# A two-layer decoder trunk on one core: the last sliding-window softmax of a layer in two halves, and the row roots by another pair of products

## The chip, the core and the metric

The kernel runs on one core of one Trainium2 chip. The time is the device time in microseconds (us) of one execution. The core has five engines that each work through a list of instructions of their own in order: PE (matrix products), DVE (vector work on tiles), ACT (functions and scaled copies), POOL (a further vector engine, which here also issues some DMAs) and SP (which only issues DMAs). They wait for each other through semaphores. PE writes its products into PSUM, which is cut into banks of 128 partitions by 512 numbers; a bank must be read out ("evicted") by DVE or ACT before PE can write new products into it.

## The reference

A trunk of two layers over one sequence of 256 tokens with 1024 channels. In each layer the normalised input is multiplied by one wide matrix, three mixers work on the pieces, each mixer's result is gated and projected back, and the sum is added to the residual:

```python
for layer in range(DEPTH):
    h = rms_norm(x, norm_w[layer])
    proj = jnp.einsum('bsd,de->bse', h, w_in[layer])
    (a_xbc, a_z, a_dt, b_q, b_k, b_v, b_z,
     c_q, c_k, c_v, c_f, c_z, gates) = jnp.split(proj, split_at, axis=-1)
    y_a = mamba2_branch(...)
    y_b = sliding_window_branch(b_q, b_k, b_v, b_z, sinks[layer], cos, sin)
    y_c = forgetting_attention_branch(...)
    ys = jnp.stack([y_a, y_b, y_c], axis=2)
    branch = jnp.einsum('bsiw,iwd->bsid', ys, w_proj[layer])
    g = jax.nn.sigmoid(gates.reshape(b, s, N_BRANCH, d) + gate_bias[layer])
    merged = jnp.sum(g * branch, axis=2)
    x = x + jnp.einsum('bsd,de->bse', merged, w_out[layer])
return rms_norm(x, final_norm_w)
```

The sliding-window mixer has 16 query heads in 4 groups, a window of 128 keys and one extra score per head (the sink) that takes part in the softmax and has no value:

```python
scores = jnp.einsum('bnqkgd,bnskd->bnkgqs', qb, kb) * (HEAD_DIM ** -0.5)
mask = band[None] & (key_pos >= 0)
scores = jnp.where(mask[None, :, None, None], scores, -jnp.inf)
probs = jax.nn.softmax(jnp.concatenate([scores, sink], axis=-1), axis=-1)[..., :-1]
out = jnp.einsum('bnkgqs,bnskd->bnqkgd', probs, vb)
```

With 256 tokens there are two query blocks of 128. The queries of block 0 see only the keys of block 0 (128 columns of scores), those of block 1 see the keys of both blocks, but never more than 128 of them at once.

## The kernel before

**Products.** To reach float32 accuracy with PE's faster number form, every weight is split in two parts, hi (a rounded copy, line 293, ACT) and lo (weight minus hi, line 294, DVE), and so is the normalised input (hTh, hTl). A weight arrives from memory by a DMA that SP issues (tile raw), in parts of 128x1024 numbers; each part costs one ACT copy and one DVE subtraction. Six raw tiles and six split tiles are in turn, and the planner lets four parts be held at a time. All products go through line 109 (mm); transposes through line 113.

**Units.** The wide matrix is worked through in units that the program text lists one after another. Three sorts matter here. A convolution or gate-path unit of 256 columns has 16 products into one bank. It is evicted by two ACT copies (lines 489 and 490), after which a DMA that POOL issues (line 491) adds one onto the other. For a convolution unit an ACT scaled copy (line 829), three DVE taps (line 832), an ACT tanh (line 838) and a DVE product (line 839) follow. A gate unit of 512 columns has 24 products and is evicted by one DVE addition of the bias (line 1102) and an ACT tanh (line 1105). A projection unit has 24 products of a mixer's split result with w_proj. These units take their banks in turn from a pool of three ("mm"); scores, transposes and small products take theirs from another pool ("mx").

**Side work.** Softmaxes, transposes and products with values are written as Python generators. A planner's clock (clock["t"]) advances with each product by an assumed cost; `yield 3.0` in a generator means that it goes on when this clock is 3 later, at the end of a unit. A `yield` therefore sets where on PE's list the next piece of side work stands. DVE's and ACT's lists follow from a scheduler that orders instructions by priority in program order and by assumed costs, except where an instruction is pinned (`issue_after` holds instructions back until a named one has been issued).

**The sliding softmax.** attn_quad (from line 586) handles four heads of one group, a quad. Its scores lie in four mx banks: columns 0:128 are block 0, columns 128:384 block 1. Block 0 takes a masked reduction per head on DVE (line 618), which also writes the tile pp, and an exponential per head on ACT (line 613). Block 1 takes a predicated copy, which folds the two key blocks into 128 columns (line 626), a maximum (line 627), a minimum with the sink for two heads (line 631), and an exponential per head. After that each block has its sink's part of the sum (lines 637 to 639), a reciprocal (641) and a product over four heads (642). Then the four transposes of block 0 with one ACT copy, `yield D_SOFT2` with D_SOFT2 = 3, the four transposes of block 1 with two DVE products (lines 678 and 679), then `yield D_EVAC`. For the second and the fourth quad the products with the values follow for two quads at once: 8 into an mx bank and 8 into an mm bank, each evicted by a DVE product with the gate path (line 726). The results are split into hi and lo again and feed the projection of this mixer.

In layer 0 the fourth quad's softmax lies at 141 to 147 us of the span, while PE works on a gate unit; ten units of 256 columns follow, and behind them the projection unit. Layer 1 does the same 395 us later.

**Row roots.** At the start of layer 0 (normalize, line 1388) each token's 1/rms must stand along the free axis. Two ACT copies (line 1392) scale the identity matrix's rows by it; two float32 products of 128 columns with a matrix of ones spread the diagonal over all partitions; four DVE products (line 1402) multiply the input by it, and four splits into hTh and hTl follow.

Of the kernel before, what the change touches and what calls it, by code (L numbers as in the profile page):

```python
# [16 lines left out]
P = 128  # L17
# [14 lines left out]
D_FOLD = 8.0  # L32
N_RAW, N_SPLIT = 6, 6
# [17 lines left out]
def hybrid_trunk(  # L51
# [238 lines left out]
    def split(hi, lo, src, scale=None, keep=lambda f: f):  # L290

        if scale is None:
            keep(act)(hi, src, AF.Copy)  # L293
            keep(tt)(lo, src, hi.bitcast(F32), op=ALU.subtract)  # L294
# [91 lines left out]
    def feed(i=-1):  # L386

        lim = state["limit"]
        while state["split"] < len(stream) and state["split"] != lim and (
# [7 lines left out]
            else:  # L397
                split(hi, lo, raw, keep=keep)
# [187 lines left out]
    def attn_quad(y, last, products, biases, nsink, v, vcols, sz, gated, scored=lambda: None, window=False):  # L586
# [29 lines left out]
        for h in range(4) if window else ():  # L616
            own = pps[0][:, h // 2, h % 2 * P:h % 2 * P + P]
            nc.vector.tensor_tensor_reduce(  # L618
                out=own, in0=scs[h][:, 0:P], in1=wmask, scale=-0.125, scalar=nsink[:, h:h + 1],
                op0=ALU.add, op1=ALU.min, accum_out=nm[:, h:h + 1])  # L620
            chances(h, 0, own)
        for h in range(4) if window else ():


            own = scs[h][:, 2 * P:3 * P]
            nc.vector.copy_predicated(own, wmask.bitcast(mybir.dt.uint32), scs[h][:, P:2 * P])
            nc.vector.tensor_reduce(nm[:, 4 + h:5 + h], own, axis=mybir.AxisListType.X, op=ALU.max)
            if h % 2 == 1:
                hs = slice(h - 1, h + 1)
                nh = slice(3 + h, 5 + h)  # L630
                stt(nm[:, nh], nm[:, nh], -0.125, nsink[:, hs], op0=ALU.mult, op1=ALU.min)
                for i in (h - 1, h):
                    chances(i, 1, scs[i][:, 2 * P:3 * P])
        for b in range(2) if window else ():
# [7 lines left out]
            tt(of_heads(b), of_heads(b), bc(rs.rearrange("p (i j) -> p i j", i=2), 3, P), op=ALU.mult)  # L642
        for p in () if window else range(2):
# [22 lines left out]
        if window:  # L666
            first, both = T("L4", [P, 2, 512]), T("L2", [P, 512])
            for b in range(2):
                if b == 1:
# [718 lines left out]
    def normalize(y):  # L1388

        rb = T("L1", [P, S])  # L1390
        for t in range(2):
            act(rb[:, t * P:(t + 1) * P], ident, AF.Copy, scale=y.rn[:, t:t + 1])
# [27 lines left out]
    with tc.manual_schedule(engines={ENG.PE, ENG.DVE, ENG.Activation, ENG.Pool}):  # L1420
# [119 lines left out]
        y0.rn = rsqrt(v, 2, r0)  # L1540

# [42 lines left out]
```

## Time and profile before

| | |
|---|---|
| median of 3 runs | 807.94 us (807.66 to 808.07) |
| the profiled execution's own time | 808.24 us |
| its span | 806.5 us (1.74 us lie around it) |
| granted TensorE clock | 0.999 |
| busy: PE, DVE, ACT, POOL | 99%, 85%, 66%, 21% |
| instructions on DVE, ACT | 1414, 1144 |

PE's busy time is counted from the start of an instruction to its modelled end, and the records of successive products overlap. So a short wait of PE is read better from the distance between the starts of two products: a product of 512 columns is followed by the next start 0.22 us later when nothing waits, one of 256 columns by 0.11 us. A row "x2" of a timeline holds two instructions that stand without idle time between them.

### The profile page before, as it was taken

To read this page: it belongs to the slowest core of one execution; us is meant where nothing else is said; L and a number is where in the kernel's file an instruction comes from. 1 tells how busy PE (TensorE), PEld (TensorE's weight loads), DVE (VectorE), ACT (ScalarE), POOL (GpSimd) and SP (SyncE) were. 2 spreads that over 40 slices of the span, in tenths; PEclk is the share of its full clock that TensorE was granted. 3 is DMA by queue.
4 is the path that set the end of the run, shared out by engine and by line. 5 is a ranking of instruction groups with operands and counts; after the bars stand their busy time and mean duration, and the time that the engine had idled before them with its cause. 6 is when DMAs were issued, how large, how long until landed. Compare 5 with 4: busy or idle time off the path is not lost.

```text
span 806.5 us, 14832 instructions
## 1 busy us (share of the span) xinstructions
PE 797.2 (99%) x5162; PEld 711.2 (88%) x5162; DVE 684.8 (85%) x1414; ACT 533.7 (66%) x1144; POOL 170.9 (21%) x238
## 2 busy tenths in 40 slices
PE   8999999999999999999999999999999999999996
PEld 7998988888888988888998899888889989888896
DVE  6868999998899997795785799999879999969865
ACT  7776768875776785543665678687747768755452
POOL 3156213130320100033001741222212110002000
PEclk9999999999999999999999999999999999999999
DMA  9998987797665565676678987689986646576632
GB/s 313 268 266 178 248 222 195 212 295 226 161 212 172 170 192 171 220 249 210 215 245 259 235 206 225 158 217 281 267 229 184 194 147 200 157 248 210 210 109 75
DMA packets 138826, 170.43 MB, mean 211 GB/s; under 512 B 9352, under 2 KB 106464, under 8 KB 138752
## 3 DMA queue, kind: packets, MB, share of 16 engines
q1 hardware_dynamic: 114960, 140.53, 55.3%
q0 software_dynamic: 13328, 13.29, 10.3%
q10 hardware_dynamic: 10464, 15.67, 6.7%
q8 instruction: 41, 0.67, 0.3%
q14 instruction: 33, 0.27, 0.1%
HBM read 154.71 MB, written 2.16 MB: 195 GB/s over the span
## 4 chain that ended last, share of the span: by engine, by line
PE 97%; DVE 1%; DMA 1%; issue 0%; ACT 0%; SPq 0%
PE mm L109 84%; PE mx L109 10%; PE mx L113 3%; DMA raw<-in_w_in_dram 1%; DVE lo L294 0%; DVE L L1102 0%; SPq L189 0%; DVE L L1446 0%; ACT L L1450 0%; ACT hi L1459 0%; ACT L L1226 0%; DVE L L1201 0%; SPq L363 0%; DVE L L1205 0%; DVE L L288 0%
## 5 line engine op out<-in xcount | busy, mean ns | idle before, releaser
L109 PE MATMUL mm<-L,hi 128*128 128x512 f32 x1056 | 354.0, 387 | 0.7 <-DVE L L1102 0.5
L294 DVE TENSOR_TENSOR lo<-raw,hi 128x1024 fp32r<-128x1024 f32 (+1 forms) x276 | 312.4, 1151 | 43.8 <-ACT hi L293 41.1
L293 ACT ACTIVATE hi<-raw 128x1024 fp32r<-128x1024 f32 (+1 forms) x276 | 265.9, 982 | 60.3 <-PE mm L109 38.2
L109 PE MATMUL mm<-hi,L 128*128 128x512 f32 (+2 forms) x1168 | 303.4, 349 | 0.1
L109 PE MATMUL mm<-L,lo 128*128 128x256 f32 x1056 | 266.6, 273 | 0.0
L109 PEld LDWEIGHTS mm<-hi,L 128*128 128x128 f32 x1168 | 205.7, 190 | 23.1 <-issue 1.5
L109 PEld LDWEIGHTS mm<-L,hi 128*128 128x128 f32 x1056 | 194.9, 190 | 27.3 <-issue 4.9
L109 PEld LDWEIGHTS mm<-L,lo 128*128 128x128 f32 x1056 | 202.1, 191 | 5.4
L109 PE MATMUL mm<-lo,L 128*128 128x512 f32 (+2 forms) x584 | 201.6, 347 | 0.0
L109 PEld LDWEIGHTS mm<-lo,L 128*128 128x128 f32 x584 | 110.2, 190 | 11.0 <-DVE lo L294 0.3
L491 POOL DMA_DIRECT2D L<-L x68 | 60.3, 911 | 191.9 <-ACT L L490 180.2
L1071 POOL TENSOR_SCALAR_AFFINE_SELECT bias<-bias 128x128 f32<-128x128 f32 x64 | 33.4, 555 | 77.2 <-DMA bias<-cumd 77.2
L832 DVE SCALAR_TENSOR_TENSOR L<-L,vec,L 128x255 f32<-128x255 f32 (+2 forms) x96 | 46.2, 481 | 2.1 <-ACT L L829 0.3
L489 ACT ACTIVATE L<-mm 128x256 f32<-128x256 f32 x84 | 32.0, 381 | 19.5 <-PE mm L109 14.1
L655 ACT ACTIVATE pp<-pp,nm 128x128 f32<-128x128 f32 x64 | 28.2, 443 | 22.1 <-DVE nm L649 22.1
L1105 ACT ACTIVATE L<-L 128x512 f32<-128x512 f32 x24 | 15.1, 630 | 35.7 <-DVE L L1102 31.2
L491 POOL DMA_DIRECT2D qt<-L x16 | 13.8, 862 | 76.3 <-ACT qt L490 76.3
L613 ACT ACTIVATE pp<-pp,nm 128x128 f32<-128x128 f32 x32 | 12.6, 394 | 25.6 <-DVE nm L618 24.9
L1138 POOL TENSOR_TENSOR L<-L,L 128x512 f32<-128x512 f32 x8 | 12.0, 1496 | 73.9 <-DVE L L1137 73.9
L490 ACT ACTIVATE L<-mm 128x256 f32<-128x256 f32 x68 | 26.2, 386 | 1.2 <-DMA L<-L 1.2
L1102 DVE TENSOR_TENSOR L<-mm,L 128x512 f32<-128x512 f32 x22 | 15.1, 686 | 11.7 <-PE mm L109 9.1
L838 ACT ACTIVATE L<-L 128x256 f32<-128x256 f32 x32 | 13.4, 418 | 16.5 <-DVE L L832 16.4
(212 smaller groups left out, 918.3 us busy)
## 6 DMA issues: line engine op xcount, KB each, us to landing
raw<-in_w_in_dram SPq DMA_DIRECT2D x191, 512.0 KB, 5.2
raw<-in_w_proj_dram SPq DMA_DIRECT2D x48, 512.0 KB, 6.2
L<-L POOLq DMA_DIRECT2D x72, 128.0 KB, 5.4
raw<-in_w_out_dram SPq DMA_DIRECT2D x16, 512.0 KB, 4.8
bias<-cumd ACTq DMA_DIRECT2D x16, 256.0 KB, 3.2
L<-cumd ACTq DMA_DIRECT2D x8, 512.0 KB, 6.5
L<-in_gate_bias_dram ACTq DMA_DIRECT2D x12, 256.0 KB, 5.9
qt<-L POOLq DMA_DIRECT2D x16, 128.0 KB, 6.0
```

What stands on the lines that cost most here:

```text
L109: nc.tensor.matmul(o, a, b, **kw)
L113: nc.tensor.transpose(o, a, i)
L293: keep(act)(hi, src, AF.Copy)
L294: keep(tt)(lo, src, hi.bitcast(F32), op=ALU.subtract)
L489: act(halves(lo), ordered(p[:, S:2 * S]), AF.Copy)
L490: last = act(halves(out), ordered(p[:, 0:S]), AF.Copy)
L491: nc.gpsimd.dma_start(out, lo, accum_op=ALU.add)
L655: act(pp[:, i, sl], pp[:, i, sl], AF.Exp, scale=-1.0, bias=nm[:, e:e + 1], accum_out=sums[:, e:e + 1])
L832: stt(a[:, s:S], x_[:, 0:S - s], y.vec[:, 16 * j + u:16 * j + u + 1], a[:, s:S], op0=ALU.mult, op1=ALU.add)
L1071: nc.gpsimd.affine_select(out=bias[:, i, dst], in_=bias[:, i, src], compare_op=ALU.is_ge, fill=NEG, base=0, pattern=[[-1, P]], channel_mul ...
L1102: tt(halves(g), p, halves(y.gb), op=ALU.add)
L1105: finish(act(g, g, AF.Tanh, scale=0.5))
```

## The change

It has two parts that do not touch each other.

The row roots: 1/rms is split in two parts (rparts: a DVE copy into the faster number form, and a DVE subtraction for the rest). Four ACT copies scale the identity by them, and two products of 256 columns with the ones in the faster form add up in one bank. The wait ahead of the products is `yield 4.0` in place of `yield 2.0`.

The softmax: in the sliding mixer's last quad of a layer (`apart`), only block 0 is computed at first. After block 0's transposes the generator waits `D_LATER` = 1.5; then block 1's part (later_block) and its normalisation are issued, held behind the latest lo split of a weight at that point; after a further `D_FOLD` = 8 come block 1's transposes. The first three quads of a layer are computed as before.

```diff
+D_LATER = 1.5
 ...
             keep(act)(hi, src, AF.Copy)
-            keep(tt)(lo, src, hi.bitcast(F32), op=ALU.subtract)
+            return keep(tt)(lo, src, hi.bitcast(F32), op=ALU.subtract)
 ...
-                split(hi, lo, raw, keep=keep)
+                state["latest"] = split(hi, lo, raw, keep=keep)
 ...
+        apart = window and last
+
+        def later_block():
+            for h in range(4):
+                own = scs[h][:, 2 * P:3 * P]
+                nc.vector.copy_predicated(own, wmask.bitcast(mybir.dt.uint32), scs[h][:, P:2 * P])
+                nc.vector.tensor_reduce(nm[:, 4 + h:5 + h], own, axis=mybir.AxisListType.X, op=ALU.max)
+                if h % 2 == 1:
+                    hs = slice(h - 1, h + 1)
+                    nh = slice(3 + h, 5 + h)
+                    stt(nm[:, nh], nm[:, nh], -0.125, nsink[:, hs], op0=ALU.mult, op1=ALU.min)
+                    for i in (h - 1, h):
+                        chances(i, 1, scs[i][:, 2 * P:3 * P])
+
+        if window:
+            if not apart:
+                later_block()
+            for b in range(1 if apart else 2):
+                normalize_block(b)
 ...
             for b in range(2):
-                if b == 1:
+                if b == 1 and apart:
+                    yield D_LATER
+                    with tc.issue_after(state["latest"].ins):
+                        later_block()
+                        normalize_block(1)
+                    yield D_FOLD
+                elif b == 1:
                     yield D_SOFT2
 ...
-        rb = T("L1", [P, S])
+        rb = [T("L1", [P, S], F32R) for _ in range(2)]
         for t in range(2):
-            act(rb[:, t * P:(t + 1) * P], ident, AF.Copy, scale=y.rn[:, t:t + 1])
-        yield 2.0
+            for o, r in zip(rb, y.rparts):
+                act(o[:, t * P:(t + 1) * P], ident, AF.Copy, scale=r.bitcast(F32)[:, t:t + 1])
+        yield 4.0
         p = pmx()
-        for t in range(2):
-            mm(p[:, t * P:(t + 1) * P], ones, rb[:, t * P:(t + 1) * P], start=True, stop=True)
+        for i in range(2):
+            mm(p[:, 0:S], onesr, rb[i], start=(i == 0), stop=(i == 1))
 ...
         y0.rn = rsqrt(v, 2, r0)
+        y0.rparts = [T("rparts", [P, 2], F32R, bufs=2) for _ in range(2)]
+        nc.vector.tensor_copy(y0.rparts[0], y0.rn[:, 0:2])
+        tt(y0.rparts[1], y0.rn[:, 0:2], y0.rparts[0].bitcast(F32), op=ALU.subtract)
```

The function normalize_block(b) holds the lines 637 to 642 of before unchanged. Line numbers of after are one higher than before up to line 612. In the softmax 618 becomes 629, 626/627/631 become 638/639/643, and 637/639/641/642 become 620/622/624/625; behind it 678/679 are 693/694, 726 is 741, 832/839 are 847/854, 940 is 955, 1102 is 1117 and 1402 is 1418.

How the lists of the engines change is shown for DVE at three places. In the rows, lo is the low part of a weight, mm and mx are PSUM banks, the number behind a name tells one tile from another, and L1, L2, L8, L16 are working tiles.

The first place is layer 0's last quad, from the gate unit's first eviction on. Before:

```order
L1102 TENSOR_TENSOR L2_409_2027<-mm_396_1942,L2_395_1940 128x512
L641 RECIPROCAL rsum_406_2005<-sums_400_1958 128x4
L639 TENSOR_TENSOR sums_400_1958<-sums_400_1958,es_407_2008 128x4
L642 TENSOR_TENSOR pp_397_1955<-pp_397_1955,rsum_406_2005 128x2x256
L641 RECIPROCAL rsum_408_2012<-sums_400_1958 128x4
L642 TENSOR_TENSOR pp_398_1956<-pp_398_1956,rsum_408_2012 128x2x256
L940 TENSOR_SCALAR L8_182_905<-L1_410_2030,L8_182_905 128x256
L294 TENSOR_TENSOR lo_419_2065<-raw_371_1837,hi_418_2064 128x1024
L294 TENSOR_TENSOR lo_422_2077<-raw_374_1851,hi_421_2076 128x1024
L294 TENSOR_TENSOR lo_437_2139<-raw_388_1914,hi_436_2138 128x1024
L1102 TENSOR_TENSOR L2_424_2082<-mm_411_2033,L2_395_1940 128x512
L294 TENSOR_TENSOR lo_440_2153<-raw_391_1928,hi_439_2152 128x1024
```

After, from the sink's part of block 0 on:

```order
L622 TENSOR_TENSOR sums_403_1965<-sums_403_1965,es_408_1994 128x4
L624 RECIPROCAL rsum_409_1998<-sums_403_1965 128x4
L625 TENSOR_TENSOR pp_400_1962<-pp_400_1962,rsum_409_1998 128x2x256
L1117 TENSOR_TENSOR L2_410_2013<-mm_399_1949,L2_398_1947 128x512
L955 TENSOR_SCALAR L8_185_912<-L1_411_2016,L8_185_912 128x256
L295 TENSOR_TENSOR lo_420_2051<-raw_374_1844,hi_419_2050 128x1024
L295 TENSOR_TENSOR lo_423_2063<-raw_377_1858,hi_422_2062 128x1024
L295 TENSOR_TENSOR lo_438_2125<-raw_391_1921,hi_437_2124 128x1024
L1117 TENSOR_TENSOR L2_425_2068<-mm_412_2019,L2_398_1947 128x512
L295 TENSOR_TENSOR lo_441_2139<-raw_394_1935,hi_440_2138 128x1024
L638 COPY_PREDICATED mx_404_1966<-wmask_9_88,mx_404_1966 128x128
L847 TENSOR_SCALAR L1_426_2071<-L1_381_1870,vec_181_901,L1_426_2071 128x255
```

Block 0 alone is now finished ahead of the first gate eviction (L1117), the three lo splits and the second eviction follow as before, and block 1's predicated copies and maxima (L638, L639) come behind the fourth lo split, among the taps of a convolution unit (L847).

The second place is around the products with the values. Before, from the products with the masks behind block 1's transposes to the eviction of the values' two banks (L726):

```order
L839 TENSOR_SCALAR L8_377_1862<-L1_443_2162,L1_430_2115 128x256
L678 TENSOR_TENSOR L4_431_2120<-mx_447_2187,other_10_89 128x512
L679 TENSOR_TENSOR L2_432_2121<-mx_447_2187,tri_5_76 128x512
L294 TENSOR_TENSOR L8_503_2449<-L8_182_905,L8_502_2448 128x2x256
L294 TENSOR_TENSOR lo_468_2294<-raw_420_2068,hi_467_2293 128x1024
L832 TENSOR_SCALAR L1_457_2228<-L1_426_2090,vec_178_894,L1_457_2228 128x255
L294 TENSOR_TENSOR L8_503_2449<-L8_182_905,L8_502_2448 128x2x256
L832 TENSOR_SCALAR L1_457_2228<-L1_426_2090,vec_178_894,L1_457_2228 128x254
L294 TENSOR_TENSOR lo_471_2308<-raw_423_2080,hi_470_2307 128x1024
L832 TENSOR_SCALAR L1_457_2228<-L1_426_2090,vec_178_894,L1_457_2228 128x253
L726 TENSOR_SCALAR L8_182_905<-mx_463_2263,L8_182_905 128x512
L726 TENSOR_SCALAR L8_182_905<-mm_464_2272,L8_182_905 128x512
```

After, from just behind the first product with a mask (L693) to the second eviction of the values (L741):

```order
L847 TENSOR_SCALAR L1_464_2258<-L1_435_2114,vec_181_901,L1_464_2258 128x254
L694 TENSOR_TENSOR L2_433_2107<-mx_475_2300,tri_5_76 128x512
L847 TENSOR_SCALAR L1_464_2258<-L1_435_2114,vec_181_901,L1_464_2258 128x253
L295 TENSOR_TENSOR lo_483_2352<-raw_442_2142,hi_482_2351 128x1024
L854 TENSOR_SCALAR L8_380_1869<-L1_474_2297,L1_464_2258 128x256
L295 TENSOR_TENSOR lo_498_2429<-raw_454_2208,hi_497_2428 128x1024
L847 TENSOR_SCALAR L1_486_2361<-L1_460_2233,vec_181_901,L1_486_2361 128x255
L741 TENSOR_SCALAR L8_185_912<-mx_487_2366,L8_185_912 128x512
L847 TENSOR_SCALAR L1_486_2361<-L1_460_2233,vec_181_901,L1_486_2361 128x254
L295 TENSOR_TENSOR lo_501_2443<-raw_457_2222,hi_500_2442 128x1024
L847 TENSOR_SCALAR L1_486_2361<-L1_460_2233,vec_181_901,L1_486_2361 128x253
L741 TENSOR_SCALAR L8_185_912<-mm_488_2375,L8_185_912 128x512
```

Between the product with the second mask and the second eviction of the values' banks stood two lo splits and three taps, and two splits of results (L294 128x2x256). Now three lo splits, four taps and one product L854 stand there, and the two evictions are no longer neighbours.

On PE the transposes of block 1 stand five units behind those of block 0 (two before), the products with the values two units after that (two before), and the projection unit two units later (four before). So the order of units is the same, and the side work stands three units later among them. On ACT the exponentials of block 1 stand two units of 256 columns later, and two DMA issues of cumd (line 861) move behind them; on POOL two DMA issues of line 491 stand ahead of the masks of the forgetting mixer (line 1071). SP's list is the same.

The third place is the normalisation at the start of layer 0. Before:

```order
L294 TENSOR_TENSOR lo_67_349<-raw_52_274,hi_66_348 128x1024
L294 TENSOR_TENSOR lo_70_367<-raw_53_276,hi_69_366 128x1024
L1402 TENSOR_TENSOR L8_23_130<-L8_23_130,mx_72_373 128x512 x3
L294 TENSOR_TENSOR L16_73_376<-L8_23_130,L16_73_376 128x4x128
L1402 TENSOR_TENSOR L8_23_130<-L8_23_130,mx_72_373 128x512
L294 TENSOR_TENSOR L16_73_376<-L8_23_130,L16_73_376 128x4x128 x3
L294 TENSOR_TENSOR lo_77_429<-raw_54_278,hi_76_428 128x1024
```

After:

```order
L295 TENSOR_TENSOR lo_70_356<-raw_54_278,hi_69_355 128x1024
L295 TENSOR_TENSOR lo_73_374<-raw_55_280,hi_72_373 128x1024
L295 TENSOR_TENSOR lo_80_436<-raw_56_282,hi_79_435 128x1024
L1418 TENSOR_TENSOR L8_23_130<-L8_23_130,mx_76_406 128x512 x3
L295 TENSOR_TENSOR L16_77_409<-L8_23_130,L16_77_409 128x4x128 x3
L1418 TENSOR_TENSOR L8_23_130<-L8_23_130,mx_76_406 128x512
L295 TENSOR_TENSOR lo_83_454<-raw_57_284,hi_82_453 128x1024
L295 TENSOR_TENSOR L16_77_409<-L8_23_130,L16_77_409 128x4x128
```

The third lo split of the next weight piece (raw_54 before, raw_56 after) stands ahead of the four products by the row roots (L1402, now L1418) instead of behind them and the four splits of the input; the fourth lo split stands ahead of the input's last one.

More of the change, by code (lines that the diff above doesn't have):

```diff
@@ L614, in chances, with normalize_block @@
                 bias=nm[:, e:e + 1], accum_out=sums[:, e:e + 1])
[L616 to L634, printed above, removed]
+        def normalize_block(b):
             hs = slice(4 * b, 4 * b + 4)
```

6 lines of the change are left out of this document (added).

## The prediction

> **What bounds the kernel now.** I read the page first, then PE's waits, then the distances between the starts of products on PE's timeline, and only where PE stands did I look at the engine that it waits for. The page's busy shares, its chain and PE's waits:
>
> ```profile
> span 806.5 us, 14832 instructions
> PE 797.2 (99%) x5162; PEld 711.2 (88%) x5162; DVE 684.8 (85%) x1414; ACT 533.7 (66%) x1144; POOL 170.9 (21%) x238
> PE 97%; DVE 1%; DMA 1%; issue 0%; ACT 0%; SPq 0%
> PE mm L109 <- DVE L L1102: 0.5, 1, 0.5
> ```
>
> PE is the bound, 97% of the chain is its own. So the time changes by the products that PE is given or spared, and by moments in which a product waits. Most of DVE's and ACT's work is free as long as it is in time. The change adds no product but in the normalisation; what it can move are PE's waits. The timeline of PE shows these beside the change, layer 0 and then layer 1:
>
> ```profile
> 150.97 0.38 PE L109 MATMUL mm<-L,hi 128*128 128x512 f32 x1
> 151.88 0.45 PE L109 MATMUL mm<-L,hi 128*128 128x512 f32 x1 [0.53 <-DVE L L1102]
> 152.17 0.38 PE L109 MATMUL mm<-L,lo 128*128 128x256 f32 x2
> ...
> 546.40 0.98 PE L109 MATMUL mm<-L,hi 128*128 128x512 f32 x2
> 547.22 0.38 PE L109 MATMUL mm<-L,lo 128*128 128x256 f32 x2
> ```
>
> With 0.22 us between starts as usual, the product at 151.88 should have started at 151.19: 0.69 us lost. In layer 1 two products with 0.22 each should bring the next row at 546.84, or 546.91 with the 0.07 by which the product at 151.88 takes longer too (0.29 to the next row): 0.31 lost. Both are the first product of a 256-column unit. Its bank was last used by the second gate unit, whose eviction (L1102) stands late in DVE's list. DVE's and ACT's timelines of layer 0 show why:
>
> ```profile
> 144.98 0.69 DVE L1102 TENSOR_TENSOR L<-mm,L 128x512 f32<-128x512 f32 x1
> 146.55 3.89 ACT L293 ACTIVATE hi<-raw 128x1024 fp32r<-128x1024 f32 x4
> 147.63 3.50 DVE L294 TENSOR_TENSOR lo<-raw,hi 128x1024 fp32r<-128x1024 f32 x3
> 151.05 0.68 DVE L1102 TENSOR_TENSOR L<-mm,L 128x512 f32<-128x512 f32 x1
> ```
>
> The softmax holds the first L1102 back to 144.98. On ACT the tanh of that eviction stands ahead of the four hi copies (146.55), the first lo needs the first copy's end (about 147.6, a quarter of 3.89 later), three lo splits take 3.42, and only then comes the second L1102; PE starts 0.83 after it.
>
> **The row roots.** Rows of PE, DVE and ACT at the start:
>
> ```profile
> 20.82 0.61 PE L109 MATMUL mx<-L,ones 128*128 128x128 f32 x4
> 21.19 0.47 PE L109 MATMUL mm<-hi,L 128*128 128x256 f32 x2
> 21.49 0.28 PE L109 MATMUL mm<-lo,L 128*128 128x256 f32 x1
> 21.60 0.39 PE L109 MATMUL mm<-hi,L 128*128 128x256 f32 x2
> ...
> 29.22 0.59 PE L109 MATMUL mm<-hi,L 128*128 128x512 f32 x2
> 29.74 0.48 PE L109 MATMUL mm<-lo,L 128*128 128x512 f32 x1
> 30.06 0.59 PE L109 MATMUL mm<-hi,L 128*128 128x512 f32 x2
> ...
> 28.47 4.75 DVE L294 TENSOR_TENSOR lo<-raw,hi 128x1024 fp32r<-128x1024 f32 x6
> ...
> L1392 ACT ACTIVATE L<-ident,rs 128x128 f32<-128x128 f32 x2 | 0.7, 402 | 0.0
> ```
>
> The two float32 products of before hold PE for 0.37 (20.82 to 21.19), and the pair behind them takes 0.30 instead of 0.22, so 0.45. The new two have 256 columns in the faster form, as the products at 21.49 have at 0.11 each: 0.22. The gain is 0.15 by the distance alone and 0.23 with the slow pair; I take 0.2. The Trainium skill ("FP8 and Floating Point Precision", TensorE Precision Notes) says that true float32 takes four passes through the array; four records for what the program writes as two products show only two for each, so the trace doesn't settle the number of passes. By four passes of 128 columns, at the 55.8 ns that "TensorE: Matmul & The Clock Gate" (Wait — 56ns) gives for one, it would be 0.45 before and 0.23 gained, an estimate at my upper value.
>
> Two more ACT copies (0.4 each) lie ahead of a hi copy, and two tiny DVE instructions ahead of the lo splits; PE needs neither within a unit, and the extra unit of delay covers them. Without that cover they would cost at most their 0.8. The moved third lo split is worth more. The row at 29.74 comes 0.52 after the one before it where two products take 0.43, and the next 0.32 after a single one where 0.22 is usual: 0.19 lost waiting for the split that starts at 28.47, behind the normalisation. After, it stands ahead of the normalisation and is long done. The next one has to follow seven normalisation instructions instead of eight and a split; I put its end at about 30.3, and PE wants it at 30.7. The early part sums to -0.39, between -0.15 (if the fourth split eats the 0.19) and -0.42.
>
> **The softmax, up to the second gate eviction.** The steps of the first block:
>
> ```profile
> 141.32 0.35 DVE L618 CUSTOM_DVE_ANT_0 pp<-mx,wmask,nsink 128x128 f32<-128x128 f32 x1
> 142.71 0.39 ACT L613 ACTIVATE pp<-pp,nm 128x128 f32<-128x128 f32 x1
> 143.09 0.39 ACT L613 ACTIVATE pp<-pp,nm 128x128 f32<-128x128 f32 x1
> ...
> 142.93 0.49 DVE L626 COPY_PREDICATED mx<-wmask,mx 128x128 f32<-128x128 uint32 x2
> 143.33 0.48 DVE L627 TENSOR_REDUCE nm<-mx 128x1 f32<-128x128 f32 x2
> 143.73 0.15 DVE L631 SCALAR_TENSOR_TENSOR nm<-nm,nsink 128x2 f32<-128x2 f32 x1
> ```
>
> Without block 1, DVE has done its four reductions by about 142.5. The exponentials follow each other by 0.38 on ACT from 141.7 on and end at about 143.4; sink, sum and reciprocal (0.5 with the handing over) and the product (0.6) bring the first L1102 to 144.5, 0.48 earlier. DVE idles there, because it waits for ACT. All that hangs on the chain moves by the same 0.48: lo splits from 147.15, second L1102 at 150.57, PE at 151.4. The stall is 0.2 instead of 0.69: a gain of 0.48.
>
> **The softmax, after that.** Here DVE pays back what it didn't do. Durations and windows:
>
> ```profile
> 152.00:165.00 13.00, 13.00 (x96) 11.25 (x97) 12.11 (x19) 10.74 (x23) 4.03 (x5) 1.00 0.97 274
> 165.00:177.00 12.00, 12.00 (x75) 10.99 (x74) 11.13 (x19) 9.45 (x20) 4.83 (x9) 1.00 1.02 300
> ...
> 155.48 1.52 DVE L832 SCALAR_TENSOR_TENSOR L<-L,vec,L 128x255 f32<-128x255 f32 x3
> 156.97 2.36 DVE L294 TENSOR_TENSOR lo<-raw,hi 128x1024 fp32r<-128x1024 f32 x2
> 159.24 0.42 DVE L839 SCALAR_TENSOR_TENSOR L<-L,L 128x256 f32<-128x256 f32 x1
> 159.58 0.68 DVE L678 TENSOR_TENSOR L<-mx,other 128x512 f32<-128x512 f32 x1
> 160.18 0.68 DVE L679 TENSOR_TENSOR L<-mx,tri 128x512 f32<-128x512 f32 x1
> ...
> 154.99 0.42 DVE L839 SCALAR_TENSOR_TENSOR L<-L,L 128x256 f32<-128x256 f32 x1 [0.55 <-ACT L L838]
> 172.58 1.23 DVE L294 TENSOR_TENSOR lo<-raw,hi 128x1024 fp32r<-128x1024 f32 x1 [0.27 <-ACT hi L293]
> 176.82 0.43 DVE L839 SCALAR_TENSOR_TENSOR L<-L,L 128x256 f32<-128x256 f32 x1 [0.54 <-ACT L L838]
> ...
> 165.77 0.42 ACT L838 ACTIVATE L<-L 128x256 f32<-128x256 f32 x1 [1.65 <-DVE L L832]
> ...
> 176.30 0.59 PE L109 MATMUL mm<-hi,L 128*128 128x512 f32 x2
> ```
>
> The columns of the windows are length, then busy time of PE, PEld, DVE, ACT and POOL. DVE is busy for 23.24 of the 25 us up to the projection unit, so it has 1.76 of slack. From one start to the next, a lo split takes 1.14, a tap 0.4 to 0.5, a product of 512 columns 0.60, L839 0.34, a predicated copy 0.20, a maximum 0.20, L631 0.15.
>
> The list of after goes on at 152.3, behind the fourth lo split: four copies, four maxima, two minima and a sink difference (2.1) with the six taps of two units (2.8) and two L839 (0.7), whose second waits for ACT, since its tanh stands behind block 1's exponentials. That gives 158.15; then sum, reciprocal and product of block 1 (0.95), so the next weight's first lo starts at about 159.15. Before, it started at 156.97: DVE is 2.2 late, because it idled while ACT did block 0 and now does block 1 where it has little slack.
>
> From 159.15 to the end of the values' second eviction (L741) I count eight lo splits (9.1), nine taps (3.6 at 0.4), two 512-wide splits, two L694-type products and two evictions (6 by 0.6, 3.6) and two L854 (0.7): 17.0, so 176.1 if nothing waits. I add 0.5 for a lo split behind its hi copy, since ACT must run a tanh and evict two units in front of it, and 0.2 for taps back to back: 176.9 with the write's tail. PE's first product of the projection unit needs this bank, and starts 0.14 later (the distance from an eviction's end to PE at 151.88): 177.03. Without any stall PE would be there at 176.30 - 0.69 = 175.61. So layer 0 loses 1.42 in place of 0.69, **+0.73**. In between PE also meets the lateness at a unit whose bank ACT evicts late and at the second value products, but these lie within the 1.42, not on top of it.
>
> Layer 1 has the same DVE list, and PE stands 0.38 later against it, the difference of 0.69 and 0.31. It loses 1.04 in place of 0.31, **+0.73** again. With no wait at all the sum is 176.33, 0.72 lost in layer 0 and 0.34 in layer 1: +0.03 each, the lower bound. With three waits as before (0.55, 0.27, 0.54) in place of my 0.7 it is 0.66 more, +1.39 each, the upper bound.
>
> The rest I cost at nothing: two DMAs of cumd go out later on ACT's queue, and POOL's masks stand behind two more DMA issues. They serve the scan and the forgetting mixer, which begin only behind the projection unit, and POOL is busy for 21%. If that cover were gone, PE would wait at the first of those mixers' products.
>
> **The sum.** -0.39 + 0.73 + 0.73 = +1.07. The profiled execution is 808.24 (span and 1.74 around it), 0.30 above the median of the runs; on the median 807.94 this gives **809.0**. About 0.2% (1.6 us) is what a measurement of this kernel can tell from no change.
>
> **The rivals.** (a) DVE keeps up: block 1's work fits into the slack and the stalls vanish in both layers, -0.69 - 0.31 - 0.39: 806.55. For it speaks that the split takes 2.2 us of DVE work out of the place where PE is waiting. Against it: the slack of 1.76 lies behind ACT's answers (the 0.54 and 0.27 waits), not where the work is put. It decides if the values' second eviction ends before 175.5. This is the faster side. (b) ACT holds the rest. Its row at 165.77 stood 1.65 idle for a DVE tap, with all evictions of units queued behind it. If DVE is later, such a wait grows, delays the eviction of PE's banks and the next hi copy, hence the next lo and the next tap. I price one such round at 0.6 per layer over mine: 810.2; it decides if a third tap ends over 0.5 later than I have it. The Trainium skill ("PSUM — Partial Sum Buffer", Engine vs sequencer instructions) calls the queues of ScalarE and VectorE strict FIFO, and the idle ahead of 165.77, with ready evictions behind it, agrees with that. (c) Only the first stall shrinks and DVE is just in time later, the lower bound of the sum: 0.06 - 0.39, 807.6.
>
> **How the numbers follow.** My forecast, with 808.4 to 809.5 as its own range, gets 0.40; (b) 0.32, since my count contains only one wait and the list has many; (c) 0.14; (a) 0.14. Slower by over 0.2% (above 809.55) takes (b) and a little of mine: 0.35. Faster by over 0.2% (below 806.3) needs more than (a) gives: 0.09. The rest is 0.56. The range from 807.0 to 810.7 leaves out most of (a) below and a second round of (b) above.
>
> **What would show it.** In the profile after: PE's products with the ones at about 23.5, twice 256 columns, no gap near 29.7; PE's stall at 151 down to 0.2; DVE with over 1 us idle between 142 and 147; the second L741 ending at about 177 with PE's first projection product right behind it, at 177.03 less the 0.39 of the early gain. I am wrong if DVE reaches that eviction before 176, or if PE waits anywhere past the projection unit.

## The result and the profile after

The changed kernel takes 809.14 us (median of 22 runs, 808.59 to 809.57), the kernel before, run beside it, 807.97 us (22 runs). The ratio is 1.0015, with a 95% interval from 1.0009 to 1.0021: slower by 0.7 to 1.7 us. The 1.17 us between the medians is under the 0.2% that the prediction set as the least that tells, but the whole interval lies above 1. The profiled execution took 808.95 us, its span is 807.2.

The page of the changed kernel:

```profile
PE 797.2 (99%) x5160; PEld 711.4 (88%) x5160; DVE 684.4 (85%) x1416; ACT 533.2 (66%) x1146; POOL 174.2 (22%) x238
PE 88%; DVE 6%; issue 2%; ACT 2%; DMA 1%; SPq 0%; ACTq 0%; DVEq 0%
```

PE's busy time is the same 797.2. But the chain now leaves PE for 12% of its length (3% before) and goes through lo splits, taps and the values' evictions: it is dragged through DVE's list. Where the time went is seen by following one and the same product through both timelines. Before and after, on PE:

```profile
12.40 0.38 PE L109 MATMUL mm<-hi,L 128*128 128x256 f32 x1
...
206.07 0.33 PE L109 MATMUL mx<-L,L 128*64 128x128 f32 x2
...
762.25 0.68 PE L109 MATMUL mm<-hi,L 128*128 128x512 f32 x2
```

```profile
12.09 0.38 PE L110 MATMUL mm<-hi,L 128*128 128x256 f32 x1
...
29.34 0.59 PE L110 MATMUL mm<-hi,L 128*128 128x512 f32 x2
...
205.89 0.33 PE L110 MATMUL mx<-L,L 128*64 128x128 f32 x2
...
762.94 0.68 PE L110 MATMUL mm<-hi,L 128*128 128x512 f32 x2
```

The first row stands ahead of the change: its 0.31 arises in the first 12 us and differs from run to run (0.13 to 0.69 in the runs below). Against it, the product at 30.06 before comes 0.40 earlier (-0.72 against -0.31): the row roots. Ahead of the softmax of layer 0 the distance is still -0.72; behind its projection, at 206, it is -0.18, so layer 0 loses 0.54. At 762 it is +0.69, so layer 1 loses 0.87. The sum is +1.01, the medians differ by 1.17.

Inside the layers, PE's timeline of the changed kernel at the places that the prediction named, first layer 0, then layer 1:

```profile
150.24 0.61 PE L110 MATMUL mm<-L,hi 128*128 128x512 f32 x2
150.69 0.39 PE L110 MATMUL mm<-L,lo 128*128 128x256 f32 x2
...
168.26 1.69 PE L110 MATMUL mm<-L,bias 128*64 128x256 f32 x16
170.29 0.48 PE L110 MATMUL mm<-L,hi 128*128 128x512 f32 x1 [0.35 <-ACT qt L491]
...
175.42 0.38 PE L110 MATMUL mm<-L,hi 128*128 128x512 f32 x1
176.02 0.48 PE L110 MATMUL mm<-hi,L 128*128 128x512 f32 x1 [0.22 <-DVE L L741]
...
564.16 1.69 PE L110 MATMUL mm<-L,bias 128*64 128x256 f32 x16
566.20 0.48 PE L110 MATMUL mm<-L,hi 128*128 128x512 f32 x1 [0.35 <-ACT qt L491]
...
571.33 0.38 PE L110 MATMUL mm<-L,hi 128*128 128x512 f32 x1
571.93 0.48 PE L110 MATMUL mm<-hi,L 128*128 128x512 f32 x1 [0.22 <-DVE L L741]
```

The stall at 151 is gone: two products of 0.22 each bring the next row 0.45 later. New are waits at the values and behind them. Before, the values' second half took 1.40 from its start to the next unit:

```profile
161.70 1.47 PE L109 MATMUL mm<-L,bias 128*64 128x256 f32 x16
163.10 0.48 PE L109 MATMUL mm<-L,hi 128*128 128x512 f32 x1
```

Now it takes 2.03 (168.26 to 170.29), 0.63 more, and the projection's first product comes 0.60 behind its forerunner instead of 0.22, 0.38 more. Both layers show the same.

DVE's and ACT's timelines of the changed kernel show both ends of the mechanism:

```profile
142.50 0.16 DVE L622 TENSOR_TENSOR sums<-sums,es 128x4 f32<-128x4 f32 x1 [0.80 <-ACT es L621]
143.52 0.68 DVE L1117 TENSOR_TENSOR L<-mm,L 128x512 f32<-128x512 f32 x1
145.20 0.43 DVE L955 SCALAR_TENSOR_TENSOR L<-L,L 128x256 f32<-128x256 f32 x1 [1.00 <-ACT L L954]
146.15 3.50 DVE L295 TENSOR_TENSOR lo<-raw,hi 128x1024 fp32r<-128x1024 f32 x3 [0.52 <-ACT hi L294]
149.56 0.68 DVE L1117 TENSOR_TENSOR L<-mm,L 128x512 f32<-128x512 f32 x1
...
158.16 3.53 DVE L295 TENSOR_TENSOR lo<-raw,hi 128x1024 fp32r<-128x1024 f32 x3
...
168.12 0.68 DVE L694 TENSOR_TENSOR L<-mx,tri 128x512 f32<-128x512 f32 x1
...
171.22 1.23 DVE L295 TENSOR_TENSOR lo<-raw,hi 128x1024 fp32r<-128x1024 f32 x1 [0.56 <-ACT hi L294]
175.28 0.69 DVE L741 SCALAR_TENSOR_TENSOR L<-mm,L 128x512 f32<-128x512 f32 x1
...
169.28 0.42 ACT L853 ACTIVATE L<-L 128x256 f32<-128x256 f32 x1 [2.24 <-DVE L L847]
169.60 0.36 ACT L490 ACTIVATE L<-mm 128x256 f32<-128x256 f32 x1
169.87 0.37 ACT L491 ACTIVATE qt<-mm 128x256 f32<-128x256 f32 x1
```

Between 142 and 147 DVE stands idle for 2.3 us waiting for ACT (0.80, 1.00, 0.52), where it was busy before. From 158.16 on it works through its list with one wait of 0.56, and finishes the values' second eviction at 175.97. PE's first projection product follows at 176.02.

The rows also show that the 0.63 at the values is two waits. 0.21 of it falls inside the second half: its third pair of products starts at 168.85, 0.37 behind the pair before it instead of 0.21 (the pair after it loses the other 0.05), and 0.05 behind the end of L694, the product with the second mask whose result the values' products read. The other 0.42 is a wait for a bank. The units' three banks go round in turn, and the values' second half takes a turn. So the unit at 170.29 needs the bank of the unit that ended at 164.36; ACT, after 2.24 of waiting for a tap, has emptied it at 170.24. Two turns later the projection needs the bank of the values themselves, which DVE empties (L741). A smaller wait for a bank that ACT empties late stands at 158.41 (0.19, in layer 1 0.11), where ACT's copies come behind block 1's exponentials. The product behind the projection's wait follows 0.32 later instead of 0.22, a further 0.10. In layer 0 these are 0.19 + 0.21 + 0.42 + 0.38 + 0.10 = 1.30, against a stall of 0.76 that went (the 0.69, and 0.07 by which the product behind it was slow): 0.54, as read above. In layer 1 they are 1.23 against 0.38: 0.85, beside the 0.87 read above.

### The profile page after: what moved, and what is told of

The parts are those of the page before. It is cut to its first block, busy times and chain, and to the rows that moved or that the text cites. A ratio compares the mean times of both kernels' runs of the same rounds, so it can differ in the third digit from the quotient of the medians.

```text
span 807.2 us, 14833 instructions
## 1 busy us (share of the span) xinstructions
PE 797.2 (99%) x5160; PEld 711.4 (88%) x5160; DVE 684.4 (85%) x1416; ACT 533.2 (66%) x1146; POOL 174.2 (22%) x238
## 4 chain that ended last, share of the span: by engine, by line
PE 88%; DVE 6%; issue 2%; ACT 2%; DMA 1%; SPq 0%; ACTq 0%; DVEq 0%
PE mm L110 76%; PE mx L110 9%; PE mx L114 3%; DVE lo L295 3%; DVE L L847 2%; DMA raw<-in_w_in_dram 1%; ACT hi L294 0%; DVE L L1117 0%; DVE L L295 0%; DVE L L854 0%; ACT L L853 0%; DVE L L693 0%; ACT pp L614 0%; DVE L L741 0%; ACT L L490 0%
## 5 line engine op out<-in xcount | busy, mean ns | idle before, releaser
L294 ACT ACTIVATE hi<-raw 128x1024 fp32r<-128x1024 f32 (+1 forms) x276 | 265.7, 982 | 56.4 <-PE mm L110 32.0
L1086 POOL TENSOR_SCALAR_AFFINE_SELECT bias<-bias 128x128 f32<-128x128 f32 x64 | 38.1, 626 | 87.0 <-DMA bias<-cumd 86.9
L847 DVE SCALAR_TENSOR_TENSOR L<-L,vec,L 128x255 f32<-128x255 f32 (+2 forms) x96 | 46.1, 480 | 1.5 <-ACT L L844 0.3
L1117 DVE TENSOR_TENSOR L<-mm,L 128x512 f32<-128x512 f32 x22 | 15.1, 686 | 11.2 <-PE mm L110 11.2
L997 POOL TENSOR_TENSOR sm<-sm,mhalf 128x8 f32<-128x8 f32 x2 | 3.4, 1684 | 95.0 <-DVE sm L995 95.0
```

Source lines behind the costliest of these rows:

```text
L847: stt(a[:, s:S], x_[:, 0:S - s], y.vec[:, 16 * j + u:16 * j + u + 1], a[:, s:S], op0=ALU.mult, op1=ALU.add)
L1086: nc.gpsimd.affine_select(out=bias[:, i, dst], in_=bias[:, i, src], compare_op=ALU.is_ge, fill=NEG, base=0, pattern=[[-1, P]], channel_mul ...
L1117: tt(halves(g), p, halves(y.gb), op=ALU.add)
```

## The experiments

Each run is compared with the kernel before on the same chip; "e2" and so on are the numbers of the runs.

**e1 and e2: each part alone.** e1 is the changed kernel with the row roots put back as they were. e2 switches the halves off:

```diff
-        apart = window and last
+        apart = False
```

> Only the softmax in halves, the row roots as before. My theory (DVE idles while ACT answers for block 0, and pays block 1 back in front of the values' second eviction): +0.54 and +0.86 us in the two layers as in the trace of the changed kernel, together about +1.4, so 809.4 us; up to 809.7 if the row roots had also helped DVE in layer 0. Rival (the two parts only cost together, because the row roots shift the lists): within 0.3 us of before.

> Only the row roots, the softmax as before. My theory: -0.2 for the products and -0.2 for the wait near 29.7, so 807.55 us; the stalls at 151 and 546 stay at 0.69 and 0.31. Rival: what is won at the start is lost again at the next place where PE waits for DVE, since DVE is no earlier there: 807.9 us, with a larger stall at 151.

Measured: e1 809.36 us beside 807.68, ratio 1.0021 (1.0012 to 1.0030); e2 807.25 beside the same 807.68, 0.9994 (0.9985 to 1.0003). So the halves cost 1.68 and the roots gain 0.43, together 1.25 against the 1.17 of the whole change. The first theory holds for the sum; 1.68 is at the upper end of its 1.4 to 1.7. In the traces, however, the parts meet at the stall at 151. In e1 it is 0.19 (the 0.2 of the prediction), and layer 0 loses 0.80; with the roots it vanished, and layer 0 lost only 0.54. In e2, where it should have stayed at 0.69, PE's timeline has

```profile
150.15 0.38 PE L110 MATMUL mm<-L,hi 128*128 128x512 f32 x1
150.77 0.45 PE L110 MATMUL mm<-L,hi 128*128 128x512 f32 x1 [0.25 <-DVE L L1117]
```

0.62 instead of 0.22, a stall of 0.40. The roots take 0.29 out of this stall, 120 us behind the place where they stand. That is followed up in e9 and e10.

**e3: block 1 in DVE's idle time.** Both parts, but block 1's softmax is issued directly behind the first gate eviction, and the extra delays go:

```diff
             for b in range(1 if apart else 2):
                 normalize_block(b)
+            if apart:
+                yield 0.0
+                with tc.issue_after(state["gate"].ins):
+                    later_block()
+                    normalize_block(1)
...
-                if b == 1 and apart:
-                    yield D_LATER
-                    with tc.issue_after(state["latest"].ins):
-                        later_block()
-                        normalize_block(1)
-                    yield D_FOLD
-                elif b == 1:
+                if b == 1:
                     yield D_SOFT2
...
-                tt(halves(g), p, halves(y.gb), op=ALU.add)
+                state["gate"] = tt(halves(g), p, halves(y.gb), op=ALU.add)
```

> Both parts, but block 1's softmax is issued directly behind the first gate eviction, into the time in which DVE idles for ACT, and its transposes stand two units behind those of block 0 again. My theory: no stall at 151 or 546, none at the values and the projection either, because DVE has no backlog: 807.97 - 1.0 - 0.4 = 806.6 us, and at most 807.2 if ACT's exponentials among the hi copies make a lo split late. Rival (DVE's load between 141 and 177 is what costs, wherever block 1 stands): 808.5 us or more, the stall moving to a lo split behind 147.

Measured: 807.43 us beside 807.68, ratio 0.9999 (0.9991 to 1.0008). Neither theory has it. The stalls at 151 and 546 are gone, as the first says, and DVE's timeline shows the copies and maxima in what was idle time:

```profile
143.26 0.68 DVE L1116 TENSOR_TENSOR L<-mm,L 128x512 f32<-128x512 f32 x1
143.86 0.48 DVE L638 COPY_PREDICATED mx<-wmask,mx 128x128 f32<-128x128 uint32 x2
144.25 0.48 DVE L639 TENSOR_REDUCE nm<-mx 128x1 f32<-128x128 f32 x2
...
145.36 0.48 DVE L638 COPY_PREDICATED mx<-wmask,mx 128x128 f32<-128x128 uint32 x2
145.75 0.48 DVE L639 TENSOR_REDUCE nm<-mx 128x1 f32<-128x128 f32 x2
```

But a new wait stands at 169.1 (0.45) and at 564.3, on PE's timeline of layer 1:

```profile
564.33 0.38 PE L110 MATMUL mm<-L,hi 128*128 128x512 f32 x1
565.60 0.48 PE L110 MATMUL mm<-L,hi 128*128 128x512 f32 x1 [0.89 <-DVE L L740]
```

1.05 us, for L740, which is the values' second eviction in that kernel's numbering. In layer 0 the values were through PE before 164, and that eviction stands at 169.04 on DVE's timeline, behind lo splits and taps. So the work of block 1 was placed well, and the values' eviction was late in the list all the same.

**e4: the transposes sooner.** The changed kernel, with block 1 still late on DVE, but its transposes and the values two units earlier on PE:

```diff
                         normalize_block(1)
-                    yield D_FOLD
+                    yield 5.0
```

> The changed kernel with 5 in place of 8 for the wait behind block 1's part, so that PE's transposes of block 1 and the products with values stand two units earlier while DVE's work for block 1 stays late. My theory: PE now waits at those transposes, about 2.6 us in layer 0 and 2.2 in layer 1 (block 1 is ready near 158.2, PE is there near 155.7), and the later stalls of 1.2 each vanish behind that: 811.5 us. Rival (the cost is only that values and projection stand too close together on PE's list): faster than the changed kernel, about 807.7 us.

Measured: 813.35 us beside 807.68, ratio 1.0077 (1.0061 to 1.0092). PE's timeline:

```profile
155.56 0.38 PE L110 MATMUL mm<-L,hi 128*128 128x512 f32 x1
158.44 0.63 PE L114 MATMUL mx<-ident,pp 128*128 128x128 f32 x4 [2.49 <-ACT qt L491]
```

PE stands for 2.7 us at the transposes (2.88 from start to start) and the like in layer 1. It is slower than the 811.5 of the first theory: in layer 0 a further 1.57 was lost in the unit behind it, which the theory had not foreseen. From 159.69 to 162.89 that unit's products stand 0.43 and 0.21 apart instead of 0.22 and 0.11, and the granted clock from 159.7 to 163.0 is 0.50, against 1.00 on both sides. So PE ran at half its clock for 3.4 us, shortly behind a wait of 2.49. In layer 1 PE waited for 2.51 and the clock stayed at 1.00; in the other profiles here, none of which has so long a wait between 17 us and the end, it never falls there. That the wait brought the half clock on is likely, but no run shows what decides it. The rival, that only the closeness of values and projection costs, is out by 5.6 us. The late transposes are needed once block 1 is late.

**e5 and e6: another bank for the second product with values.** One edit, on e3 (e5) and on the changed kernel (e6); the pool of the units has three banks, that of scores and transposes five:

```diff
-zip(quads, (pmx, pmm))]
+zip(quads, (pmx, pmx if window and last else pmm))]
```

> The kernel of e3 with one more edit: in the last quad of a layer, the second product with the values takes its bank from the pool of the scores and transposes instead of the pool of the units, so no unit waits for its late eviction. My theory: the waits of 0.45 us (169.1) and 1.05 us (564.3) of e3, which the trace puts down to that eviction, vanish, and nothing else changes: 807.43 - 1.5 = 805.9 us, at most 806.4. Rival (DVE is behind anyway, the wait moves to the split results that the projection reads): 807.0 us or more.

> The changed kernel with the same one edit on the bank of the second product with values. My theory: both waits behind the values (0.41 at 169.7 and 0.38 at 175.4, and their like in layer 1) are waits for banks of the units' pool, which now has one user less between them; they vanish, and 0.2 to 0.3 at the second product with values stays: 809.14 - 1.5 = 807.6 us. Rival (DVE's lateness itself stops PE, whatever the bank): the wait moves to the projection's first products for the split results, 808.7 us or more.

Measured: e5 806.26 us beside 807.76, ratio 0.9981 (0.9973 to 0.9990); e6 807.06 beside the same, 0.9992 (0.9983 to 1.0001). Both waits of e3 are gone, and e5 is the fastest of all kernels here, 1.5 us below the kernel before. In e6 the two waits for banks behind the values vanish as well, with DVE as late as in the changed kernel. Its DVE timeline still has

```profile
168.29 0.69 DVE L694 TENSOR_TENSOR L<-mx,tri 128x512 f32<-128x512 f32 x1
...
171.40 1.22 DVE L295 TENSOR_TENSOR lo<-raw,hi 128x1024 fp32r<-128x1024 f32 x1 [0.56 <-ACT hi L294]
...
175.46 0.68 DVE L741 SCALAR_TENSOR_TENSOR L<-mx,L 128x512 f32<-128x512 f32 x1
```

and the page's chain is

```profile
PE 98%; DMA 1%; DVE 0%; ACT 0%; SPq 0%; issue 0%
```

ACT is as late, too: the copies that stood at 169.60 and 169.87 stand at 169.79 and 170.05, but the unit behind the values starts at 170.06 without waiting for them, since its bank came one turn earlier. So most of the lateness reached PE through the turn that the values took in the units' pool. Not all of it: the third pair of the values' second half starts at 169.04, right behind L694's end (168.98) and 0.22 late, as the expectation had said, and the unit at 158.58 waits 0.19 as before. With their like in layer 1, 0.41 and 0.32 us stay. Against its own kernel before, e6 is 0.70 faster where the changed kernel is 1.17 slower: the bank alone is worth 1.87 us in it.

**e11: the bank alone.** The same edit on e2.

> The row roots alone with the bank of the second product with values taken from the other pool; softmax as before the change. A control for e5 and e6. My theory: in this kernel no unit waits for the values' eviction, and the gate's bank is the one that is late, before the values come; so the edit does nothing by itself and the stalls at 151 and 546 stay: as e2 within 0.3 us, 807.3 us. Rival (the edit is a gain by itself of the size seen in e5 and e6): 806.3 us.

Measured: 807.38 us beside 807.94, ratio 0.9995 (0.9986 to 1.0004), 0.56 below its kernel before as e2 was 0.43 below its own. The stalls at 151 (0.42) and 545 (0.34) are there. The edit is no gain of its own; it takes away most of what the late softmax brings.

**e7: only the normalisation late.** PE's list is that of the changed kernel, but block 1's copies, maxima and exponentials stand with block 0:

```diff
-            if not apart:
-                later_block()
+            later_block()
...
-                        later_block()
                         normalize_block(1)
```

> The changed kernel, but block 1's copies, maxima, minima and exponentials stand with block 0 as before the change; only its sink, sum, reciprocal and product (0.95 us of DVE instead of about 3) stay behind the fourth lo split. PE's list is that of the changed kernel. My theory: the backlog of DVE at the values falls by about 2 us, so the waits behind them vanish, while the stall at 151 stays near the 0.40 of e2: 807.3 us, as e2. Rival (the late place of transposes, values and projection on PE's list costs by itself): 808.5 us or more.

Measured: 807.32 us beside 807.76, ratio 0.9996 (0.9987 to 1.0005). The stalls at 150.1 (0.40) and 545.3 (0.30) are those of e2, and no wait is left behind the values. With the same late place of transposes, values and projection on PE's list, nothing is lost: what the waits measure is block 1's late work on DVE and ACT, not that place.

**e8: the products' form without their place.** The row roots alone, with 2 in place of 4 for the wait.

> Only the row roots, with 2 in place of 4 for the wait ahead of the products, so only the form of the products changes and not their place. My theory: PE gains 0.2 us at the products and the wait near 29.7 stays at 0.19. Rival (the four ACT copies ahead of the products make PE wait for them without the extra unit): PE stands at the products for 0.5 us or more.

Measured: one time, 807.20 us; the profile is what counts. PE's timeline:

```profile
20.13 0.40 PE L110 MATMUL mx<-L,ones 128*128 128x256 f32 x2
20.37 0.38 PE L110 MATMUL mm<-hi,L 128*128 128x256 f32 x2
...
28.32 0.59 PE L110 MATMUL mm<-hi,L 128*128 128x512 f32 x2
28.84 0.48 PE L110 MATMUL mm<-lo,L 128*128 128x512 f32 x1
29.16 0.59 PE L110 MATMUL mm<-hi,L 128*128 128x512 f32 x2
```

The products take 0.24 instead of 0.37, and the pair behind them 0.22 instead of 0.30: 0.21 gained. The wait near 29 is still there (0.52 and 0.32 as before). So the form is worth 0.2, as predicted, and the rival is out. The 0.19 of the place is less sure. The wait is there when the place stays, as the prediction said, but in e1 and e10, where the row roots stand as before the change, it is missing: in e1 the products at 28.96, 29.18 and 29.61 follow each other by 0.22 and 0.43. What differs is ACT's wait for a weight from memory just ahead of the split of the input, in the kernel before

```profile
23.84 1.06 ACT L293 ACTIVATE hi<-raw 128x1024 fp32r<-128x1024 f32 x1 [0.57 <-DMA raw<-in_w_in_dram]
```

0.35 in e8, and nothing in e1 and e10. So the 0.19 goes with a late weight here, and in the profile of the changed kernel that weight is not late. How often it is, and what the new place gains on the whole, is not shown.

**e9 and e10: where the 0.29 at 151 comes from.** In e2 and e8 DVE and ACT have the same order around 138 as before, and yet ACT's tanh of a convolution unit starts 0.28 sooner behind its tap. Before, in e9 and in e10, with the DVE taps and the ACT tanh of each:

```profile
136.60 1.51 DVE L832 SCALAR_TENSOR_TENSOR L<-L,vec,L 128x255 f32<-128x255 f32 x3
138.48 0.42 ACT L838 ACTIVATE L<-L 128x256 f32<-128x256 f32 x1 [0.88 <-DVE L L832]
```

```profile
137.36 1.51 DVE L832 SCALAR_TENSOR_TENSOR L<-L,vec,L 128x255 f32<-128x255 f32 x3
138.96 0.42 ACT L838 ACTIVATE L<-L 128x256 f32<-128x256 f32 x1 [0.60 <-DVE L L832]
```

```profile
136.19 1.52 DVE L832 SCALAR_TENSOR_TENSOR L<-L,vec,L 128x255 f32<-128x255 f32 x3
138.08 0.42 ACT L838 ACTIVATE L<-L 128x256 f32<-128x256 f32 x1 [0.89 <-DVE L L832]
```

The edit of e9 and, with `nc.vector.tensor_copy` in place of `act`, of e10:

```diff
         y0.rn = rsqrt(v, 2, r0)
+        spare = T("spare", [P, 4], bufs=1)
+        for i in range(2):
+            act(spare[:, 2 * i:2 * i + 2], y0.rn[:, 0:2], AF.Copy)
```

> The kernel before with two tiny ACT copies more (128x2, into a tile that nobody reads) behind the row roots' computation; nothing of the change itself. In e2 and e8 ACT's tanh near 138 starts 0.10 us after the tap that it waits for, and before the change 0.37 after it, with the same rows around it on both engines' lists; that is worth 0.29 of the stall at 151. Theory (the place of ACT's instructions in its stream decides that 0.28): the stall at 151 is 0.40 as in e2. Rival (it goes with the earlier start of the work): it stays at 0.69.

> The kernel before with two tiny DVE copies more (128x2, into a tile that nobody reads) at the same place, where DVE has gained two instructions by the change. Theory (the place of DVE's instructions in its stream decides the 0.28 at the tap): the stall at 151 is 0.40. Rival: it stays at 0.69.

Measured: e9 808.80 us and e10 807.86, one time each. In e9 the tanh starts 0.09 behind the taps' end (137.36 + 1.51), and the stall at 151.7 is 0.41; in e10 the tanh is 0.37 behind, and the stall 0.71. In e9 all work is some 0.8 us later than before at this place, since the copies delay PE at the products with the ones by 0.8; so an earlier start is not what does it. Two more instructions on ACT are enough, two on DVE are not. All thirteen profiles agree: 0.37 in the kernel before, e1 and e10, 0.09 or 0.10 in the ten kernels with two more ACT copies. The release itself is not late. ACT has a separate instruction that waits for the tap, and it ends 0.05 behind the tap in all of them; the step from there to the tanh is 0.32 in the three and 0.04 or 0.05 in the ten. Why ACT was 0.28 late at that one place before is left open: in the trace nothing but the tap releases it, and layer 1 has no such delay.

## Why the prediction was right, and where its terms were off

**The total.** 809.14 against 809.0; +1.17 against +1.07. The likeliest case came true, and no rival. Part of the closeness is luck: in the trace layer 0 came out 0.19 below its +0.73, by the tanh that the prediction did not foresee, and layer 1 0.14 above it.

**The row roots,** -0.39: -0.40 in the trace of the changed kernel. The -0.43 of e2's times is no second measurement of it, since these hold the 0.29 at 151 as well; e2's trace is 0.70 faster behind the first 12 us. The 0.2 for the products' form is what e8 shows. The 0.19 for the place of the third lo split was read from one execution in which a weight came late, and e1 and e10 lack the wait without the new place. With the slow pair behind them the products held PE for 0.45 and now hold it for 0.24, a gain of 0.21. That is nearer to the 0.23 estimated by the four passes of the Trainium skill ("FP8 and Floating Point Precision", TensorE Precision Notes) than to the 0.15 of the bare distance, but the 0.37 from the first of them to the next product is less than the 0.45 of that estimate, so the number of passes stays open. The fourth lo split ended at 29.92, and there was no stall there.

**The first stall,** 0.69 to 0.2: it went to nothing. The chain from the first gate eviction to the second kept its length as said (6.04 from 143.52 to 149.56; 6.07 before). What the prediction did not have is that the tanh at 138 loses its 0.28 by the two added ACT instructions, so that all of DVE's list of layer 0 starts 0.28 sooner against PE. In e1, without them, the stall is the predicted 0.2.

**DVE's backlog.** The prediction let the next weight's first lo split start at 159.15 on the old clock and the values' second eviction end at 176.9. Measured: 158.16 and 175.97. DVE's first reduction of this softmax moved from 141.32 to 140.33, by 0.99, so on the old clock these are 159.15 and 176.96. The one wait of 0.5 that was put in for a lo split behind its hi copy is the 0.56 at 171.22.

**The losses behind it.** 1.42 in layer 0 became 1.23, and 1.04 in layer 1 became 1.18, seen from the net +0.54 and +0.87 and the stalls of 0.69 and 0.31 that went. In layer 0 the 0.28 of the tanh accounts for the smaller loss (1.42 - 0.28 = 1.14). In both layers the prediction left out the 0.10 by which the product behind the projection's wait is slow, though it had read 0.07 of the same kind at 151. Nearly all the rest is as it said: since PE has to wait for L741 in any case, the earlier waits lie within the loss and not on top of it. The mechanism was named rightly, a bank that waits for L741. What the prediction did not see is that the largest earlier wait, the 0.42 for a bank that ACT empties, comes from the same turn that the values take in the units' pool, so that one edit (e6) removes both and leaves 0.41 and 0.32.

**Rivals.** (a) fell: DVE did not keep up. (b), ACT holding the rest, is partly there, since ACT stood 2.24 for a tap and then evicted a unit late (the 0.35 at 170.29), but within the counted sum. The unit that it then evicted (169.60) had ended at 164.36, so a ready eviction stood behind the waiting tanh for all of the 2.24. That agrees with the strict order that the Trainium skill ("PSUM — Partial Sum Buffer", Engine vs sequencer instructions) gives for ACT's queue. The row at 165.77, by which the prediction argued, does not show it: there the next eviction was of a unit whose products ended only at 165.99, and it was not ready. (c), that the first stall shrinks and DVE is in time later, fell too; nothing is lost behind the softmax only where block 1's work was placed otherwise (e5, with the bank, and e7).

## What to carry to other kernels

Taking work out of the place where an engine holds up PE is only a gain if that engine can use the time at once; here DVE idled for 2.3 us on ACT's answers and met the same work again where it had no slack. Before moving work, ask which bank or buffer its lateness will hold, and give late results a bank from a pool that the bound engine's next units don't need: that one edit turned 1.17 us of loss into 0.70 of gain, and with block 1 in DVE's idle time into 1.5. And count the list of the second engine to the next such bank, instruction by instruction: sums of start-to-start distances held within 0.1 us over 35 us here.

## What was not expected of the hardware

Two tiny instructions more on ACT's list, at 18 us, made one tanh at 138 us start 0.28 us sooner behind the tap that releases it (0.09 and 0.10 us behind it in e9 and e8, 0.37 in the kernel before and in e10), with the same instructions around it. A difference of a few tenths between two kernels can thus come from what stands much earlier in an engine's list, and not from what the edit says; what it is in that place remains open.

In e4 PE ran for 3.4 us at a granted clock of 0.50 shortly behind a wait of 2.49, which cost 1.57 us more; after a wait of 2.51 in the other layer it did not.
